# Two raw weight buffers freed in a transformer block: the second pair of each down product loads into four tiles of another pool

## The chip, the cores and the metric

The kernel runs on one core of one Trainium2 chip. The metric is the device time of one execution in microseconds. The kernel before took 1124.71 us, the median of three runs.

## What is computed

A model of two layers over 512 tokens of width 1024, in float32. Each layer has a mixing half (a gated spatial product in the first layer, attention with a forget gate in the second, both beside an attention over 256 memory rows) and a feed-forward half. Only the feed-forward half is touched:

```python
f = rmsnorm(h, ln_ffn_pre[layer])
f = (jax.nn.silu(f @ w_ffn_gate[layer]) * (f @ w_ffn_up[layer])) @ w_ffn_down[layer]
h = h + rmsnorm(f, ln_ffn_post[layer])
```

The hidden width is 2816, which is 22 blocks of 128.

## The kernel before, in words

**Parts.** Every float32 weight or activation that goes through TensorE is split into a high part (a cast on ScalarE, `whi`) and a low part (a subtraction on VectorE, `wlo`), both at line 239, and each product is three matmuls (lines 191 to 193): high by high, high by low, low by high.

**Gate and up blocks.** The first two hidden blocks are computed plainly. The other twenty are taken two at a time. For each two, a gate block and then an up block is computed by Strassen's scheme (class `Seven`): seven half-size products instead of eight. A block loads two raw weight tiles of 128x1024 (512 KB each, line 144), forms sums of their quarters on VectorE (lines 1041 to 1046), splits seven quarters or sums into parts, and runs the seven products into three banks of PSUM, named `a`, `e` and `x`. The first is product 1 into `a`, then come product 7 (which uses the sum `s3` of line 1041) into `e` and product 2 into `x`, and then the others.

**Down blocks.** Hidden blocks are grouped by four: blocks 2 to 5, 6 to 9, 10 to 13, 14 to 17. After each of these four groups a down block (`down_sevens`) multiplies the four hidden blocks, as two pairs, by the down weights, again by Strassen's scheme, once for the first pair (`a`) and once for the second (`b`). With two layers that makes eight down blocks. The last group, 18 to 21, is multiplied by other code. Each pair loads two raw tiles of 512 KB (line 1189), in which 1 KB runs of the weights lie; VectorE forms sums in place (lines 1196 to 1201), and seven products follow. Results are added to eight accumulator tiles `ys` of 128x512 in three ways: chained in PSUM, added by VectorE from PSUM (`final`, line 1226), or copied to SBUF by ScalarE (line 1221) and added by an accumulating DMA that GpSimd issues (`put`, line 1223, tile names `y<-yo`, 256 KB each, ten in a down block). The last two additions of `final`, for `shared`, go to accumulator tiles that `put` has added to before, so they must wait for those DMAs (the third and the fifth of the ten) to land.

**Buffers.** All raw weights go through one tag of four buffers:

```python
raw = wp.tile([P, 1024], F32, tag="raw", name=name("raw"), bufs=4)
```

A gate block holds two, an up block two, the pairs of a down block two each. A buffer is free again when the last part has been split from it. Separately, the pool `plain` has twelve tiles of 128x512 float32 (one tag, `y`); during the feed-forward half `ys` holds eight of them. In the first layer the four others hold the memory rows of the second layer (`mem`, four loads of 256 KB, line 345) from the beginning of the groups on.

**Order.** A scheduler fixes the order of the instructions on each engine and on SyncE's queue when the program is built. Loads of weights are all issued by SyncE, in one queue and in that order; a load that waits for its buffer holds up those behind it. Engines take their instructions strictly in order too.

I call the place where TensorE goes over from a down block to the gate block behind it a seam, and number the eight seams in order of time: one to four in the first layer (near 260, 325, 393 and 455 us), five to eight in the second (near 857, 920, 984 and 1047 us).

Of the kernel before, what the change touches and what calls it, by code (L numbers as in the profile page):

```python
# [7 lines left out]
F32 = mybir.dt.float32  # L8
# [7 lines left out]
P = 128  # L16
# [24 lines left out]
def hybrid(ctx: ExitStack, tc: tile.TileContext, i: dict, out: bass.AP):  # L41
    nc = tc.nc
# [4 lines left out]
    wp = ctx.enter_context(tc.tile_pool(name="weights", bufs=4))  # L47
# [5 lines left out]
    last_load, last_exp, last_parts = [None], [None], [None, None]  # L53

    def name(s):
        n_of[s] = n_of.get(s, 0) + 1
        return f"{s}_{n_of[s]}"
# [4 lines left out]
    def plain(s, shape=(P, T), dt=F32):  # L62
        return yp.tile(list(shape), dt, tag="y", name=name(s))

    def prob(s, shape=(P, T)):
        return tp.tile(list(shape), F32, tag="p", name=name(s), bufs=6)

    def temp(s, shape=(P, T), tag="t", bufs=4, dt=F32):
        return tp.tile(list(shape), dt, tag=tag, name=name(s), bufs=bufs)
# [4 lines left out]
    def ps(tag, shape=(P, T), s="ps"):  # L74
        return pp.tile(list(shape), F32, tag=tag, name=name(s), bufs=2 if tag == "tr" else 3)
# [1037 lines left out]
    def feed_forward(layer, phase, xp, meanwhile=None):  # L1113
# [41 lines left out]
        class Inner:  # L1155

            def __init__(self, k, aside):
                self.k, self.aside, self.u = k, aside, {}
# [22 lines left out]

        class DownSeven:

            def __init__(self, pair):
                self.x = pair.x
                raws = []
                for dh in range(2):
                    raw = wp.tile([P, 1024], F32, tag="raw", name=name("raw"), bufs=4)
                    last_load[0] = nc.sync.dma_start(
                        raw.rearrange("p (m c) -> p m c", m=4),  # L1190
                        i["w_down"][layer, 4 * dh : 4 * dh + 4, :, pair.k : pair.k + 2, :].rearrange("m p k c -> p m (k c)"))
                    raws.append(raw.rearrange("p (m k c) -> p m k c", m=4, k=2))
                a11, a12, a21, a22 = (r[:, :, x, :] for r in raws for x in range(2))
                self.w = {4: a22}
                s3 = temp("s3").rearrange("p (m c) -> p m c", m=4)
                V.tensor_sub(s3, a11, a21)
                self.w[1] = self.parts(a11)
                V.tensor_add(a21, a21, a22)
                self.w[2] = self.parts(a12)
                V.tensor_sub(a11, a11, a21)  # L1200
                V.tensor_add(a12, a11, a12)
                self.w.update({3: a12, 5: a21, 6: a11, 7: s3})
# [14 lines left out]
        def down_sevens(pairs):  # L1217

            def put(x, *where):
                some = prob("yo")  # L1220
                A.copy(some, x)  # L1221
                for tb, dh in where:
                    G.dma_start(ys[tb][dh], some, accum_op=ALU.add)  # L1223

            def final(x, tb, dh):
                V.tensor_add(ys[tb][dh], x, ys[tb][dh])  # L1226

            a, b = DownSeven(pairs[0]), None
            chain = [ps("tr", s="yc") for _ in range(2)]
            a.product(chain, 1, True, False)  # L1230
            lows = [ps("mm", s="yl") for _ in range(2)]
            a.product(lows, 2, True, False)
            shared = [ps(t, s="ys") for t in ("mm", "lg")]
            a.product(shared, 7, True, False)
            ups = [ps(t, s="yu") for t in ("lg", "lg")]
            a.product(ups, 3, True, False)
            b = DownSeven(pairs[1])
            b.product(chain, 1, False, True)
            for x in range(2):
                put(chain[x], (x, 0))  # L1240
            b.product(shared, 7, False, True)
            for x in range(2):
                put(shared[x], (x, 1), (x + 2, 1))
            for u in (a, b):
                u.product(chain, 6, False, u is b)
            for x in range(2):
                A.copy(shared[x], chain[x])
            b.product(ups, 3, False, True)
            for x in range(2):
                final(ups[x], x + 2, 0)  # L1250
            a.product(chain, 5, False, False)
            a.product(shared, 4, False, False)
            b.product(lows, 2, False, True)
            for x in range(2):
                final(lows[x], x, 0)
            b.product(chain, 5, False, True)
            for x in range(2):
                put(chain[x], (x + 2, 0), (x + 2, 1))
            b.product(shared, 4, False, True)
            for x in range(2):  # L1260
                final(shared[x], x, 1)
# [11 lines left out]
        a, close = boundary(phase, G_MIX_POST + layer, G_FFN_PRE + layer, nnorm, rb, first, evac_first, scaled)  # L1273
# [12 lines left out]
        for gi, (k0, k1) in enumerate(groups):  # L1286
            fs, pairs = [], []
            for m in range(k0, k1, 2):
                if meanwhile and m == k1 - 2 and gi == len(groups) - 1:
                    next(meanwhile)  # L1290
                if gi < len(groups) - 1:
                    pairs.append(Inner(m, m < k1 - 2))
                else:
                    fs += [(act("fhi"), act("flo")) for _ in range(2)]
                sevens((lambda: Seven(xs, lambda n: i["w_gate"][layer, m + n], "mm", gate_rows),
                        lambda: Seven(xs, lambda n: i["w_up"][layer, m + n], "lg",
                                      lambda row, t: up_rows(row, t, fs, pairs and pairs[-1]))), m == 2, m == k0)
            nk = k1 - k0
            if gi == len(groups) - 1:
                if layer:  # L1300
                    with behind([gates[2]]):
                        A.preload_act_table_set("natural_log_exp_and_others")
                if meanwhile:
                    next(meanwhile)

                eps = small("eps")
                V.tensor_mul(eps, nnorm.r4, nnorm.r4)
                V.reciprocal(eps, eps)
                V.tensor_scalar_mul(eps, eps, RMS_EPS)
                return tail_of(fs, lambda kp, dh, aside, k0=k0: down_weights(layer, k0 + 2 * kp, dh, aside), ys, eps,  # L1310
                               layer == 1)
            down_sevens(pairs)
# [300 lines left out]
```

## Time and profile before

| what | value |
|---|---|
| three runs | 1121.97, 1124.71, 1125.1 us |
| profiled execution, own time | 1122.91 us |
| its span, first to last instruction | 1121.2 us |
| mean granted TensorE clock | 0.991 |
| busy: TensorE, VectorE, ScalarE, GpSimd | 97%, 87%, 67%, 10% |
| moved by DMA | 143.84 MB, 128 GB/s on average |

A profile names instructions by engine (PE is TensorE, PEld its weight loads, DVE VectorE, ACT ScalarE, POOL GpSimd, SP SyncE), by line of the kernel and by the program's tile names. A busy TensorE is not the same as a TensorE at full pace, since matmuls overlap. The waits view adds up the idle time of an engine by what ended it: total, times, longest. The chain of waits follows the work that ended last back from the last instruction, at each step to what released it.

### The profile page before, as it was taken

What the parts mean: (1) busy time and instruction counts of PE and PEld (TensorE: products, weight loads), DVE (VectorE), ACT (ScalarE), POOL (GpSimd) and SP (SyncE); (2) the same over time, 40 slices, a digit from 0 to 9 for tenths busy, and PEclk for the clock granted to TensorE, in tenths of its full rate; (3) what the DMA queues carried; (4) which work ended last, traced back from release to release, by engine and by line L of the source; (5) the groups of instructions that cost most, each with busy time, mean ns of one, the idle gap of its engine ahead of it and who ended that gap; (6) DMA issues with size and microseconds to landing.
All of it is one profiled execution on the core that took longest, in us unless ns stands there. A gap on an engine that the chain in (4) does not pass through costs nothing.

```text
span 1121.2 us, 19822 instructions
## 1 busy us (share of the span) xinstructions
PE 1089.7 (97%) x7267; PEld 988.8 (88%) x7267; DVE 973.3 (87%) x1942; ACT 753.6 (67%) x1588; POOL 107.4 (10%) x136
## 2 busy tenths in 40 slices
PE   9999999998989999999999999999998999999998
PEld 8998889988979898898988998889997979898896
DVE  7879769998989999897968889869998989999886
ACT  7776668665656567577746788878666656666554
POOL 0000000012030112101000000000003030111200
PEclk9999999999989999999999999999999999999999
DMA  7422331338484564746222654431238464573732
GB/s 271 154 76 75 103 106 53 116 82 205 130 180 121 136 184 95 202 136 191 62 90 60 156 132 121 139 113 39 76 95 206 132 157 132 121 194 93 195 127 76
DMA packets 77849, 143.84 MB, mean 128 GB/s; under 512 B 6772, under 2 KB 41608, under 8 KB 77752
## 3 DMA queue, kind: packets, MB, share of 16 engines
q1 hardware_dynamic: 63032, 116.57, 33.3%
q0 software_dynamic: 14016, 25.70, 13.0%
q8 instruction: 57, 0.93, 0.4%
q10 hardware_dynamic: 704, 0.32, 0.1%
q14 instruction: 40, 0.33, 0.1%
HBM read 105.23 MB, written 2.10 MB: 96 GB/s over the span
## 4 chain that ended last, share of the span: by engine, by line
PE 68%; DVE 14%; DMA 11%; ACT 4%; issue 2%; POOL 1%; SPq 0%; DVEq 0%; ACTq 0%
DMA y<-yo 6%; DVE wlo L239 5%; PE y L191 4%; PE y L192 4%; PE y L193 4%; PE ps L191 4%; PE ps L193 4%; PE ps L192 4%; PE a L191 3%; PE a L192 3%; PE a L193 3%; PE e L193 3%; PE e L192 3%; PE e L191 3%; DMA raw<-in_w_down 3%; PE x L192 2%
## 5 line engine op out<-in xcount | busy, mean ns | idle before, releaser
L239 ACT CAST whi<-raw 128x512 fp32r<-128x512 f32 x492 | 287.0, 620 | 130.1 <-DVE raw L1045 46.7
L239 DVE TENSOR_TENSOR wlo<-raw,whi 128x512 fp32r<-128x512 f32 x492 | 321.0, 683 | 21.5 <-ACT whi L239 20.8
L191 PE MATMUL x<-xshi,whi 128*128 128x256 f32 x320 | 91.7, 287 | 2.0 <-DVE y L1226 1.4
L193 PE MATMUL a<-xshi,wlo 128*128 128x256 f32 x320 | 90.4, 283 | 2.0 <-DVE wlo L239 1.9
L192 PE MATMUL x<-xslo,whi 128*128 128x256 f32 x320 | 90.8, 284 | 0.0
L193 PE MATMUL x<-xshi,wlo 128*128 128x256 f32 x320 | 90.5, 283 | 0.0
L191 PE MATMUL a<-xshi,whi 128*128 128x256 f32 x320 | 89.9, 281 | 0.0
L192 PE MATMUL a<-xslo,whi 128*128 128x256 f32 x320 | 89.8, 281 | 0.0
L1223 POOL DMA_DIRECT2D y<-yo x80 | 69.4, 1149 | 211.4 <-ACT yo L1221 189.4
L191 PE MATMUL ps<-xshi,whi 128*128 128x256 f32 (+1 forms) x224 | 68.4, 305 | 0.0
L192 PE MATMUL ps<-xslo,whi 128*128 128x256 f32 (+1 forms) x224 | 66.7, 298 | 0.0
L193 PE MATMUL ps<-xshi,wlo 128*128 128x256 f32 (+1 forms) x224 | 66.3, 298 | 0.0
L191 PEld LDWEIGHTS x<-xshi,whi 128*128 128x128 f32 x320 | 61.3, 192 | 3.6 <-DVE y L1226 3.6
L193 PE MATMUL e<-t3hi,wlo 128*128 128x256 f32 x160 | 47.9, 299 | 16.7 <-DVE wlo L239 16.7
L193 PEld LDWEIGHTS a<-xshi,wlo 128*128 128x128 f32 x320 | 60.3, 188 | 3.2 <-DVE wlo L239 3.0
L193 PEld LDWEIGHTS x<-xshi,wlo 128*128 128x128 f32 x320 | 61.4, 192 | 0.0
L192 PEld LDWEIGHTS x<-xslo,whi 128*128 128x128 f32 x320 | 61.3, 192 | 0.0
L192 PEld LDWEIGHTS a<-xslo,whi 128*128 128x128 f32 x320 | 60.2, 188 | 0.4
L191 PEld LDWEIGHTS a<-xshi,whi 128*128 128x128 f32 x320 | 60.2, 188 | 0.4
L239 ACT CAST whi<-s 128x512 fp32r<-128x512 f32 x56 | 34.8, 621 | 37.0 <-DVE s L1041 30.1
L191 PE MATMUL y<-whi,mixedhi 128*128 128x512 f32 x128 | 51.3, 401 | 0.0
L192 PE MATMUL y<-wlo,mixedhi 128*128 128x512 f32 x128 | 50.6, 395 | 0.0
(352 smaller groups left out, 3584.7 us busy)
## 6 DMA issues: line engine op xcount, KB each, us to landing
raw<-in_w_gate SPq DMA_DIRECT2D x44, 512.0 KB, 3.9
raw<-in_w_up SPq DMA_DIRECT2D x44, 512.0 KB, 4.8
raw<-in_w_down SPq DMA_DIRECT2D x44, 512.0 KB, 4.6
y<-yo POOLq DMA_DIRECT2D x80, 256.0 KB, 6.7
raw<-in_w_out SPq DMA_DIRECT2D x16, 512.0 KB, 3.7
flo<-s POOLq DMA_DIRECT2D x16, 256.0 KB, 3.3
raw<-in_w_b_q SPq DMA_DIRECT2D x8, 512.0 KB, 4.3
raw<-in_w_a_v SPq DMA_DIRECT2D x6, 512.0 KB, 8.2
```

The costliest lines, as they stand in the source:

```text
L191: PE.matmul(o, w[0], x[0], start=start, stop=False, skip_group_check=more)
L192: PE.matmul(o, w[0], x[1], start=False, stop=False, skip_group_check=more)
L193: return PE.matmul(o, w[1], x[0], start=False, stop=stop, skip_group_check=more)
L239: last_parts[:] = A.copy(hi, src), (eng or V).tensor_sub(lo, src, hi)
L1223: G.dma_start(ys[tb][dh], some, accum_op=ALU.add)
```

## The change

The second pair of each down block no longer takes two raw buffers of 128x1024. It takes four tiles of 128x512 from the pool `plain`, one for each quarter of the weights, and loads them by four DMAs of 256 KB instead of two of 512 KB. In the DRAM tensor the two hidden blocks of a pair lie side by side, so a load of both reads runs of 1 KB and a load of one reads runs of 512 B. The arithmetic is the same.

```diff
-            def __init__(self, pair):
+            def __init__(self, pair, spare):
                 self.x = pair.x
-                raws = []
-                for dh in range(2):
...
-                a11, a12, a21, a22 = (r[:, :, x, :] for r in raws for x in range(2))
+                if spare:
+                    a11, a12, a21, a22 = (plain("wd").rearrange("p (m c) -> p m c", m=4) for _ in range(4))
+                    for n, a in enumerate((a11, a12, a21, a22)):
+                        last_load[0] = nc.sync.dma_start(
+                            a, i["w_down"][layer, 4 * (n // 2) : 4 * (n // 2) + 4, :, pair.k + n % 2, :].rearrange("m p c -> p m c"))
+                else:
+                    raws = []
...
-            a, b = DownSeven(pairs[0]), None
+            a, b = DownSeven(pairs[0], False), None
...
-            b = DownSeven(pairs[1])
+            b = DownSeven(pairs[1], True)
```

The lines omitted under `else` are the old ones, indented. From here on in the file, line numbers grow by six (the first pair's load is line 1195, the sum `s3` of a pair line 1202, `put` line 1229, `final` line 1232).

SyncE's queue around the second down block, before: the first pair's two loads (3907, 3909), the second pair's (3964, 3966), then the next gate block's and up block's two each.

```order
L1189 DMA raw_3907<-in_w_down 128x4x256
L1189 DMA raw_3909<-in_w_down 128x4x256
L1189 DMA raw_3964<-in_w_down 128x4x256
L1189 DMA raw_3966<-in_w_down 128x4x256
L144 DMA raw_4103<-in_w_gate 128x1024
L144 DMA raw_4105<-in_w_gate 128x1024
L144 DMA raw_4240<-in_w_up 128x1024
L144 DMA raw_4242<-in_w_up 128x1024
```

The same place now. The four loads named `wd` are the third down block's second pair; the second down block's own stand one group earlier, at the same place behind the first down block.

```order
L1195 DMA raw_3911<-in_w_down 128x4x256
L1195 DMA raw_3913<-in_w_down 128x4x256
L144 DMA raw_4111<-in_w_gate 128x1024
L144 DMA raw_4113<-in_w_gate 128x1024
L144 DMA raw_4248<-in_w_up 128x1024
L1189 DMA wd_4752<-in_w_down 128x4x128
L1189 DMA wd_4753<-in_w_down 128x4x128
L144 DMA raw_4250<-in_w_up 128x1024
L1189 DMA wd_4754<-in_w_down 128x4x128
L1189 DMA wd_4755<-in_w_down 128x4x128
```

The gate loads have moved up to the buffers of the up block before the down block, the up loads to those of the first pair, and the second pair's loads to a whole group earlier, behind the first and the second up load. In the fourth down block of the first layer, where no down block of this kind follows, the four `mem` loads stand in the place of the four `wd` loads; in the last down block of the second layer nothing does.

VectorE's order at the second seam, before: the gate block's sum `s3` (line 1041), then parts and sums, with the two additions of `shared` (line 1226) in the middle.

```order
L1041 TENSOR_TENSOR s_13_4112<-raw_4103,raw_4105 128x512
L239 TENSOR_TENSOR wlo_4115<-raw_4103,whi_4114 128x512
L1043 TENSOR_TENSOR raw_4105<-raw_4105 128x512
L239 TENSOR_TENSOR wlo_4120<-raw_4103,whi_4119 128x512
L1226 TENSOR_TENSOR y_2472<-ys_3940,y_2472 128x512
L1226 TENSOR_TENSOR y_2474<-ys_3941,y_2474 128x512
L1045 TENSOR_TENSOR raw_4103<-raw_4105,raw_4103 128x512
L239 TENSOR_TENSOR wlo_4139<-s_13_4112,whi_4138 128x512
```

And now:

```order
L1041 TENSOR_TENSOR s_13_4120<-raw_4111,raw_4113 128x512
L239 TENSOR_TENSOR wlo_4123<-raw_4111,whi_4122 128x512
L1043 TENSOR_TENSOR raw_4113<-raw_4113 128x512
L239 TENSOR_TENSOR wlo_4128<-raw_4111,whi_4127 128x512
L1232 TENSOR_TENSOR y_2472<-ys_3944,y_2472 128x512
L1232 TENSOR_TENSOR y_2474<-ys_3945,y_2474 128x512
L1045 TENSOR_TENSOR raw_4111<-raw_4113,raw_4111 128x512
L239 TENSOR_TENSOR wlo_4147<-s_13_4120,whi_4146 128x512
```

Nothing has moved there: the two additions still stand ahead of the low part of `s3`, which the product into `e` needs.

More of the change, by code (lines that the diff above doesn't have):

```diff
@@ L1182, in feed_forward @@
         class DownSeven:
-            def __init__(self, pair):
+            def __init__(self, pair, spare):
                 self.x = pair.x
-                raws = []
-                for dh in range(2):
[L1188 to L1192, printed above, removed]
-                a11, a12, a21, a22 = (r[:, :, x, :] for r in raws for x in range(2))
+                if spare:
[5 more added lines that the diff above has]
+                    raws = []
+                    for dh in range(2):
+                        raw = wp.tile([P, 1024], F32, tag="raw", name=name("raw"), bufs=4)
+                        last_load[0] = nc.sync.dma_start(
+                            raw.rearrange("p (m c) -> p m c", m=4),
+                            i["w_down"][layer, 4 * dh : 4 * dh + 4, :, pair.k : pair.k + 2, :].rearrange("m p k c -> p m (k c)"))
+                        raws.append(raw.rearrange("p (m k c) -> p m k c", m=4, k=2))
+                    a11, a12, a21, a22 = (r[:, :, x, :] for r in raws for x in range(2))
                 self.w = {4: a22}
```

## Prediction

> **What bounds the kernel now.** I read the page first, then the waits, then the chain of waits, and then the timeline at one seam.
>
> ```profile
> PE 1089.7 (97%) x7267; PEld 988.8 (88%) x7267; DVE 973.3 (87%) x1942; ACT 753.6 (67%) x1588; POOL 107.4 (10%) x136
> ```
>
> TensorE is the bound, so only what makes it wait can be won. Its weight loads (PEld) show those waits best: total, times, longest.
>
> ```profile
> PEld e L193 <- DVE wlo L239: 18.5, 9, 3.3
> ...
> PEld x L191 <- DVE y L1226: 3.6, 8, 0.9
> ...
> PEld a L193 <- DVE wlo L239: 3.0, 5, 0.9
> ```
>
> And VectorE's, for which TensorE waits there:
>
> ```profile
> DVE s L1041 <- DMA raw<-in_w_gate: 21.6, 10, 3.3
> ...
> DVE y L1226 <- DMA y<-yo: 7.3, 6, 2.2
> ...
> DVE s L1196 <- DMA raw<-in_w_down: 2.6, 7, 0.7
> ```
>
> `e`, `x` and `a` are the three banks of a gate block, and the longest wait, for the low part of `s3` into `e`, comes once at each seam:
>
> ```profile
> 267.43 0.39 PE L193 MATMUL e<-t3hi,wlo 128*128 128x256 f32 x1 [1.61 <-DVE wlo L239]
> 331.65 0.58 PE L193 MATMUL e<-t3hi,wlo 128*128 128x256 f32 x1 [3.10 <-DVE wlo L239]
> 396.19 0.39 PE L193 MATMUL e<-t3hi,wlo 128*128 128x256 f32 x1 [1.16 <-DVE wlo L239]
> 459.75 0.51 PE L193 MATMUL e<-t3hi,wlo 128*128 128x256 f32 x1 [1.91 <-DVE wlo L239]
> 860.45 0.38 PE L193 MATMUL e<-t3hi,wlo 128*128 128x256 f32 x1 [1.83 <-DVE wlo L239]
> 923.64 0.39 PE L193 MATMUL e<-t3hi,wlo 128*128 128x256 f32 x1 [2.04 <-DVE wlo L239]
> 987.40 0.39 PE L193 MATMUL e<-t3hi,wlo 128*128 128x256 f32 x1 [1.05 <-DVE wlo L239]
> 1050.46 0.58 PE L193 MATMUL e<-t3hi,wlo 128*128 128x256 f32 x1 [2.67 <-DVE wlo L239]
> ```
>
> The eight add up to 15.4 us; with 3.6 (`x`) and 3.0 (`a`), 0.8 a seam, the seams cost TensorE 22.0 us of waiting. The change removes the gate load from this. But the chain of waits, from which I take each seam's DMA link (start, length) and one link of the second pair's load, says that the gate load is last at only two seams:
>
> ```profile
> 253.89 11.51 DMA y<-yo
> ...
> 299.99 4.69 DMA raw<-in_w_down
> ...
> 317.74 11.88 DMA y<-yo
> ...
> 384.27 6.78 DMA raw<-in_w_gate
> ...
> 446.53 11.18 DMA y<-yo
> ...
> 847.30 11.12 DMA y<-yo
> ...
> 910.68 10.91 DMA y<-yo
> ...
> 975.63 6.72 DMA raw<-in_w_gate
> ...
> 1037.68 10.74 DMA y<-yo
> ```
>
> At the other six it is the fifth accumulating DMA of the down block. VectorE's timeline at the second seam shows how:
>
> ```profile
> 324.41 0.69 DVE L1041 TENSOR_TENSOR s<-raw,raw 128x512 f32<-128x512 f32 x1 [2.49 <-DMA raw<-in_w_gate]
> ...
> 329.71 0.69 DVE L1226 TENSOR_TENSOR y<-ys,y 128x512 f32<-128x512 f32 x1 [2.20 <-DMA y<-yo]
> ```
>
> VectorE waits for the gate load, then works, then stands 2.20 us in line 1226 because the DMA has landed only then; `s3`'s low part is two operations behind, and TensorE starts at 331.65. Without the first wait VectorE reaches line 1226 2.49 us sooner and stands there 2.49 us longer. So the question is when the accumulating DMAs land.
>
> **The loads that go beside them.** SyncE's queue at this seam:
>
> ```profile
> 315.98 1.51 SPq L144 DMA_DIRECT2D raw<-in_w_gate  x2
> 318.35 3.92 SPq L144 DMA_DIRECT2D raw<-in_w_up  x2
> 334.04 1.00 SPq L144 DMA_DIRECT2D raw<-in_w_gate  x2
> ```
>
> The first four are 2 MB in 6 us (the last two are for the second gate block), beside the third to sixth accumulating DMA. Afterwards the gate's 1 MB goes out a down block earlier, into the up block's buffers, and the same place holds the up's 1 MB (pieces of 4 KB) and the next second pair's 1 MB (pieces of 512 B): the same bytes at about the same times. What the pieces' size does is seen in three stretches: 236 to 238 us (loads of 1 KB pieces), 322 to 328 (4 KB pieces) and 330 to 333 (no loads). Columns: pieces, MB, share of the 16 DMA engines; q0 is the accumulating queue, q1 SyncE's.
>
> ```profile
> q0 software_dynamic: 133, 0.25, 67.4%
> q1 hardware_dynamic: 243, 0.25, 40.7%
> ```
>
> ```profile
> q0 software_dynamic: 355, 0.65, 59.0%
> q1 hardware_dynamic: 294, 1.09, 48.4%
> ```
>
> ```profile
> q0 software_dynamic: 332, 0.60, 111.1%
> ```
>
> The accumulating queue moves 0.20 MB/us alone, 0.125 beside 1 KB pieces and 0.108 beside 4 KB pieces. The third to fifth DMA are 0.786 MB: 7.3, 6.3 and 3.9 us.
>
> **The sum, part by part.**
>
> *Second pair's load.* It is now in its tiles a group earlier; the seven waits of line 1196 (2.6 us) go. They lie on the chain (the link at 299.99 is one of them), ahead of the accumulating DMAs' issue, and VectorE has no other wait there: -2.6, bounds 0 and -2.6. The operations on the new tiles are the same 128x512; I cost them at nothing.
>
> *Gate load.* Its wait (21.6 us) goes, but pays only where it is last or where the next link moves too.
>
> *Seams one, two, five, six.* Worth what the fifth DMA lands earlier. Beside the up's 4 KB pieces nothing changes. Beside 512 B pieces I have no row: if as many pieces pass per accumulating piece as at 1 KB (1.8), the loads take half as much from the queue, 0.16 MB/us is left and 4.9 us needed, 2.5 less; if as many bytes pass, 6.3 us, 1.0 less. Half of the loads are such pieces, so 1.2 or 0.5; the row nearest is the one of 1 KB pieces, read by pieces: 1.2 each, -4.8. Bounds: 0, and 3.4 (as if alone).
>
> *Seams three and seven.* Line 1226 has six waits for DMA, so here none, and the gate load is last. The e-wait goes until the accumulating DMA takes its place; with 1.2 earlier nearly all of 1.16 + 0.8 and 1.05 + 0.8: I take 1.35 each, -2.7. Bounds: 0.5 and 1.9.
>
> *Seam four.* The `mem` loads (2 KB pieces) take the place of the `wd` loads: half of 1.2, -0.6.
>
> *Seam eight.* No `wd` loads follow, so half of the loads beside the accumulating DMAs are gone: half-way between 7.3 and 3.9 us, 1.7; with the loads over before the fifth DMA begins, a little more: -2.0.
>
> *Clock.* Some of the waits cost twice. These stretches hold four of the seams; columns are TensorE's busy time, granted clock, DMA share, GB/s.
>
> ```profile
> 325.00:337.00 12.00, 8.48 (x46) 0.72 1.06 243
> 455.00:464.00 9.00, 6.91 (x41) 0.81 1.07 221
> 918.00:928.00 10.00, 7.60 (x46) 0.83 1.07 222
> 1047.00:1054.00 7.00, 4.33 (x23) 0.76 1.14 226
> ```
>
> With a clock of one half for part of each, that is 6.7, 3.4, 3.4 and 3.4 us at half clock; TensorE works through some 15 of them and loses 7.5. It happened behind e-waits of 1.91, 2.04, 2.67 and 3.10 us, not behind 1.61 and 1.83. Now the waits for `a` and `x` (0.8) merge into the e-wait: single waits of 1.6 + 0.8 - 1.2 = 1.2, 2.7, 2.1, 1.4 and 1.6 us remain at seams one, two, four, five, six, and 1.5 at eight. Two stay above 1.9, at 1.7 each: 3.4 of 7.5 lost, and for the phase of the window I keep one more: -2.4. The Trainium skill (TensorE: Matmul & The Clock Gate, "Part 1: The HAM clock gate") has the clock fall after an idle window of about 3.4 us that runs free; here 1.91 us was enough once. By the page no remaining wait would halve it and the sum would be 5.1 lower.
>
> Together 2.6 + 4.8 + 2.7 + 0.6 + 2.0 + 2.4 = 15.1 us. From the profiled execution's own 1122.9 that gives 1107.8; the median of the runs lies 1.8 above the profiled one, so 1109.6, say **1109 us**.
>
> **Cover.** The `wd` loads stand in SyncE's one queue between the two up loads and ahead of the second gate block's. Their own waits (tiles split late in the down block) hold those up. The up's second load now needs a buffer of the first pair, free earlier than the second pair's that it waited for, and its block comes only behind the gate block; the second gate block's loads went out at 334.04, 12 us behind the seam's last. Both covers are longer than the 3.5 us that the 128 small pieces of one engine take at 27 ns (worked out below). If the cover failed, the wait of line 1041 would be in the up block instead.
>
> **The rivals.**
>
> *All of it goes.* Many small pieces pass while the accumulating queue is still empty, and the rest cost it next to nothing: the fifth DMA lands 3.4 us earlier, no wait is left, no half clock. 2.6 + 22.0 + 7.5 = 32: 1092.6. For it: the row of 1 KB pieces already shows the queue gaining. Against: the up's 4 KB pieces stay. Chance 0.12.
>
> *Nothing lands earlier.* The same 2 MB go beside the DMAs; the gate load was hidden anyway. Then the second pair's 2.6, seam eight's 2.0 and its half clock 1.7, and 0.5 each at three and seven remain, 7.3, less two new half clocks of 1.7 at seams one and five, where the merged waits are 2.4 and 2.6 us: 3.9, 1120.8. Chance 0.22.
>
> *Slower.* The small pieces go in groups: SyncE's queue keeps an engine for many pieces before the accumulating queue has its turn. A 1 KB piece took 40.7% of 32 us over 243, 54 ns, a 4 KB piece 158 ns; a 512 B piece is then some 27 ns, and beyond six in a group a turn is dearer than beside 4 KB. With thirteen in a group (0.35 us) the 128 `wd` pieces of an engine are ten turns, each 0.2 us longer; what is left then goes alone, and the fifth DMA lands 1.5 us later at six seams: 9 us, and half clock at all of these, 7 more, less 2.6 and seam eight's 3.7: 1134. Against: beside 1 KB pieces only 1.8 passed per turn. Chance 0.11. The Trainium skill (DMA: Bandwidth & Descriptors, "Queues, rings and completion order") says so: an engine drains a packet of typically 9 to 17 descriptors from one queue before it switches; by the row above the trace does not agree for 1 KB pieces, and no row has 512 B ones.
>
> That the tiles are not free and the change does nothing is excluded: the loads stand a group ahead.
>
> **How the numbers follow.** The forecast has 0.55. Its own range is 1097 (the fifth DMA 2.5 us earlier: 10.0 + 3.8 + 1.2 + 2.5 + 2.6 + 7.5 = 27.6) to 1115 (0.5 earlier: 2.0 + 1.6 + 0.3 + 2.0 + 2.6 + 1.0 = 9.5). The range of 8 in 10 takes in nothing landing earlier and half of the way to all going: 1094 to 1123. A measurement of this kernel tells about 0.3% from no change, 3.4 us, so faster begins below 1121.3. The case at 1120.8 lies on that edge; a third of it counts as faster, the rest as the same. Faster 0.55 + 0.12 + 0.08 = 0.75, same 0.14, slower 0.11.
>
> **What would show it.** Right: line 1041 no longer waits at a seam and line 1196 not at all; line 1226 waits at five or six seams, 2 to 4 us each, and the chain has `y<-yo` links there that are about 1 us shorter; beside `wd` pieces the accumulating queue moves over 0.108 MB/us; one to three stretches of half clock. Wrong: the links are as long as now or longer, line 1226 has taken over the whole of the 21.6 us, and the half clock has come to more seams; or the line 1041 waits have moved to the up blocks.

## The result and the profile after

| kernel | median us | runs | ratio to the kernel before | 95% interval |
|---|---|---|---|---|
| before | 1124.9 | 1121.97 to 1126.37 | | |
| changed | 1107.84 | 1105.52 to 1110.95 | 0.9853 | 0.982 to 0.9886 |
| changed, once more (e5), beside other experiments | 1104.83 | 1103.97 to 1110.45 | 0.9814 | 0.978 to 0.9848 |

Each ratio is to the kernel before as it was measured beside the same group of runs (its median was 1128.61 us beside e1 to e4, 1125.51 beside e5 to e8 and 1127.02 beside e9 to e11), so ratios compare better than medians. For e5 a ratio of 0.982 to 0.989 was expected; it came out just below.

The forecast was 1109 us, with a range of 1094 to 1123. The profiled execution of the changed kernel has an own time of 1105.52 us, a span of 1103.8 (17.4 less than before) and a granted clock of 0.995.

The page's first row, TensorE's waits and VectorE's waits, of the changed kernel:

```profile
PE 1082.3 (98%) x7266; PEld 986.1 (89%) x7267; DVE 972.7 (88%) x1942; ACT 752.5 (68%) x1588; POOL 107.5 (10%) x136
```

```profile
PEld e L193 <- DVE wlo L239: 14.0, 7, 3.2
```

```profile
DVE y L1232 <- DMA y<-yo: 13.1, 7, 3.4
...
DVE s L1041 <- DMA raw<-in_w_gate: 1.8, 2, 0.9
```

TensorE's busy time fell from 1089.7 to 1082.3 with the same matmuls. Some 2.4 us of that is the clock (worked out below), since a matmul at half clock is busy for longer; the rest must be waits too short for the page to count as idle, for by the start times of the matmuls (also below) the two kernels differ only at the seams and in the down blocks. The rows for `x` (3.6) and `a` (3.0) are gone, `e` went from 18.5 to 14.0. On VectorE the 21.6 us for the gate load became 1.8, the 2.6 of the second pair's load have no row any more, and the wait for the accumulating DMAs rose from 7.3 to 13.1: part of the old wait was only moved.

The e-waits, seam by seam, from TensorE's timeline (seams seven and eight have none now):

```profile
265.06 0.39 PE L193 MATMUL e<-t3hi,wlo 128*128 128x256 f32 x1 [0.57 <-DVE wlo L239]
327.62 0.58 PE L193 MATMUL e<-t3hi,wlo 128*128 128x256 f32 x1 [2.74 <-DVE wlo L239]
390.08 0.39 PE L193 MATMUL e<-t3hi,wlo 128*128 128x256 f32 x1 [0.89 <-DVE wlo L239]
452.90 0.39 PE L193 MATMUL e<-t3hi,wlo 128*128 128x256 f32 x1 [2.96 <-DVE wlo L239]
850.96 0.39 PE L193 MATMUL e<-t3hi,wlo 128*128 128x256 f32 x1 [1.57 <-DVE wlo L239]
913.32 0.39 PE L193 MATMUL e<-t3hi,wlo 128*128 128x256 f32 x1 [2.50 <-DVE wlo L239]
```

They add up to 11.2 us, against 15.4 + 6.6 before. (The row of 14.0 us is that of the weight loads; its seventh wait lies inside the last group of the first layer, at 487 us.) Two of them are longer than before (seams four and six, 1.91 and 2.04 there), which fits if the small waits for `x` and `a` in front of them are counted too: these merged into the one wait that is left.

At the seams the chain of waits has these DMA links now (start, length):

```profile
254.38 8.63 DMA y<-yo
315.02 10.56 DMA y<-yo
378.62 9.43 DMA y<-yo
440.05 10.81 DMA y<-yo
839.33 9.59 DMA y<-yo
900.91 10.37 DMA y<-yo
```

All are the fifth accumulating DMA. At five of the six seams where it was on the chain before, the links are 0.4 to 2.9 us shorter; at seam three it has taken the gate load's place; at seven and eight there is no such link. VectorE at the second seam:

```profile
319.12 0.69 DVE L1041 TENSOR_TENSOR s<-raw,raw 128x512 f32<-128x512 f32 x1
...
321.86 0.69 DVE L1232 TENSOR_TENSOR y<-ys,y 128x512 f32<-128x512 f32 x1 [0.24 <-PE ys L193]
325.68 0.69 DVE L1232 TENSOR_TENSOR y<-ys,y 128x512 f32<-128x512 f32 x1 [3.12 <-DMA y<-yo]
```

Line 1041 waits for nothing, and line 1232 stands for 3.12 us where it stood for 2.20: of the 2.49 us that VectorE no longer waits for the gate load, 0.92 come back here.

### The profile page after: what moved, and what is told of

It is laid out like the page before. It is cut to its first block, busy times and chain, and to the rows that moved or that the text cites. A ratio compares the mean times of both kernels' runs of the same rounds, so it can differ in the third digit from the quotient of the medians.

```text
span 1103.8 us, 19831 instructions
## 1 busy us (share of the span) xinstructions
PE 1082.3 (98%) x7266; PEld 986.1 (89%) x7267; DVE 972.7 (88%) x1942; ACT 752.5 (68%) x1588; POOL 107.5 (10%) x136
## 3 DMA queue, kind: packets, MB, share of 16 engines
q0 software_dynamic: 14016, 25.70, 13.1%
## 4 chain that ended last, share of the span: by engine, by line
PE 77%; DVE 10%; DMA 6%; ACT 3%; issue 2%; POOL 1%; SPq 0%; DVEq 0%; ACTq 0%
DMA y<-yo 5%; PE y L191 5%; PE y L192 5%; PE y L193 4%; PE a L191 4%; PE a L192 4%; PE a L193 4%; PE ps L191 4%; PE ps L193 4%; PE ps L192 4%; PE e L193 3%; DVE wlo L239 3%; PE e L192 3%; PE e L191 3%; PE x L192 3%; PE x L193 3%
## 5 line engine op out<-in xcount | busy, mean ns | idle before, releaser
L239 ACT CAST whi<-raw 128x512 fp32r<-128x512 f32 x444 | 260.4, 619 | 116.1 <-DVE raw L1045 46.2
L239 DVE TENSOR_TENSOR wlo<-raw,whi 128x512 fp32r<-128x512 f32 x444 | 291.9, 687 | 20.4 <-ACT whi L239 19.8
L239 ACT CAST whi<-s 128x512 fp32r<-128x512 f32 x56 | 34.8, 622 | 24.6 <-DVE s L1041 15.4
## 6 DMA issues: line engine op xcount, KB each, us to landing
wd<-in_w_down SPq DMA_DIRECT2D x32, 256.0 KB, 10.5
```

Source lines behind the costliest of these rows:

```text
L239: last_parts[:] = A.copy(hi, src), (eng or V).tensor_sub(lo, src, hi)
```

## The experiments

**Theory.** A seam ends when the fifth accumulating DMA lands, and the loads that share the 16 DMA engines with it set when. The change gained by freeing the gate load, by what the loads now leave to that DMA, and by fewer stretches of half clock. **Rivals.** Only the freed buffers matter; or the queue of small pieces is harmful; or the DMA's issue, not its neighbours, sets the landing.

| run | edit to the changed kernel | median us | ratio | 95% interval |
|---|---|---|---|---|
| e1 | `wd` loads later | 1098.74 | 0.9727 | 0.9693 to 0.976 |
| e2 | up loads held | 1134.3 | 1.0057 | 1.0033 to 1.008 |
| e3 | order of the accumulating DMAs | 1092.55 | 0.9674 | 0.9649 to 0.97 |
| e4 | up loads in 512 B pieces | 1099.54 | 0.9733 | 0.9706 to 0.976 |
| e6 | kernel *before* with the order of e3 | 1111.17 | 0.9857 | 0.9825 to 0.9888 |
| e7 | second pair late again | 1125.61 | 1.0 | 0.9979 to 1.002 |
| e8 | TensorE kept busy in three waits | 1109.47 | 0.9846 | 0.9821 to 0.987 |
| e9 | the same, products in the old order | 1109.01 | 0.9849 | 0.9808 to 0.989 |
| e10 | e1 and e3 together | 1090.0 | 0.9671 | 0.965 to 0.9692 |
| e11 | e10 and `mem` loads later | 1089.11 | 0.9664 | 0.9639 to 0.9689 |

e1 to e4 ran beside one another, then e6 to e8 beside the changed kernel's second measurement (0.9814), then e9 to e11. One thousandth is 1.1 us.

### e1: the wd loads out of the way

```diff
-                        last_load[0] = nc.sync.dma_start(
-                            a, i["w_down"][...])
+                        with behind([loads[-3]]):
+                            last_load[0] = nc.sync.dma_start(
+                                a, i["w_down"][...])
```

`loads` lists the loads of gate and up blocks; the third from the end is the second gate block's last.

> The changed kernel with the four wd loads issued behind the second gate block's loads, so that no 512 B piece goes beside the accumulating DMAs at seams one to three and five to seven; the mem loads at seam four stay. Theory (a seam ends when the fifth accumulating DMA lands, and the loads that share the 16 DMA engines with it set when): the e-waits of 0.73, 2.90, 1.05, 1.73 and 2.66 us at seams one, two, three, five and six become nearly nothing, as at seam eight where no wd load stands now, and two of the three stretches of half clock (1.7 us each) go: 9.1 + 3.4 = 12.5 us less than the changed kernel, about 1095; seam four keeps its 3.1. Rival (the up block's 4 KB pieces hold the DMA, not the wd loads, or its issue by GpSimd does): nothing moves, 1106 to 1110.

Measured: 1098.74 us. TensorE's and VectorE's waits:

```profile
PEld e L196 <- DVE wlo L242: 10.1, 8, 3.6
```

```profile
DVE y L1236 <- DMA y<-yo: 9.5, 8, 3.4
```

The e-wait at seam two fell from 2.7 to under 0.9 us and at seam six from 2.5 to 0.4; at seam four, where the `mem` loads stayed, it is the 3.6. One stretch of half clock is left, at seam four, and the median time from issue to landing of the `y<-yo` DMAs fell from 7.4 to 5.6 us. The link of the second seam, which began at 315.02 us and was 10.56 long, is now this:

```profile
314.71 8.58 DMA y<-yo
```

It begins 0.3 us earlier and ends 2.3 earlier: the neighbours of the DMA set its landing, and the rival that its issue does is excluded. The time fell by less than expected (about 1095). VectorE still waits 0.8 to 1.2 us for the DMA at seams two, three, five and six, and at seam three the e-wait did not fall at all (0.89 to 1.10); that the 4 KB pieces are the cause of what stays is argued, not shown.

### e2: the up loads held

```diff
+        if y is not None:
+            G.tensor_copy(raw[:, :1], y[:, :1])
```

`y` is the tile of the last addition of line 1232 (`ys[1][1]`).

> The changed kernel with the first up block's loads of a group held until the last addition of line 1232 before it has been made (a one-column copy by GpSimd into the raw tile, which is then overwritten, reads that accumulator tile and the load waits for the copy). The wd loads then stand ahead of the up loads in SyncE's queue, beside the accumulating DMAs as now. Theory: only 512 B pieces are left beside the third to fifth accumulating DMA, at 0.164 MB/us for 0.786 MB, 4.8 us, against some 5.8 now (half beside 4 KB pieces at 0.108, half at 0.164): 1.0 less at five or six seams, 0.7 at the first, and one or two stretches of half clock, 1.7 each: 1099 to 1102. Rival (the wd loads alone hold the DMA): 1106 to 1110.

Measured: 1134.3, a miss of over 30 us. The wait for `y<-yo` has gone from VectorE's list, as the theory has it, but ScalarE and TensorE show what came instead:

```profile
ACT whi L241 <- DMA raw<-in_w_up: 44.6, 9, 6.3
```

```profile
PEld a L193 <- ACT s L1073: 17.3, 8, 3.4
...
PEld a L195 <- DVE wlo L241: 11.3, 11, 1.7
```

At the second seam the held loads were issued at 331.60 us, and ScalarE stood up to 6.3 us for them. The parts of the up block are made well ahead of its products; a load that is in time for TensorE is late for the engines that work ahead. This is a cover that my prediction had counted as long ("its block comes only behind the gate block"): from TensorE's side it is, from ScalarE's it isn't. About the pieces this run tells nothing.

### e3: the two awaited DMAs first

```diff
             for x in range(2):
-                put(shared[x], (x, 1), (x + 2, 1))
+                put(shared[x], (x, 1))
+            for x in range(2):
+                G.dma_start(ys[x + 2][1], yo[x], accum_op=ALU.add)
```

> The changed kernel with the four accumulating DMAs of shared issued in the order of use: both that line 1232 waits for as the third and the fourth, the two others as the fifth and the sixth. Theory: the queue moves one DMA after the other, so the one that is waited for lands one DMA of 262 KB earlier, 1.6 us at 0.164 MB/us to 2.4 us at 0.108; the e-waits of 0.73, 2.90, 1.05, 3.12, 1.73 and 2.66 us lose 0.73, 1.8, 1.05, 1.8, 1.7 and 1.8, 8.9 together, and the three stretches of half clock 3 to 5: 12 to 14 us less, about 1095. Rival (the DMAs in the queue share the engines and land close together): under 0.3 us a seam, 1106 to 1108.

Measured: 1092.55, 0.9674. The waits and the second seam:

```profile
PEld e L193 <- DVE wlo L239: 5.1, 4, 1.6
```

```profile
324.89 0.69 DVE L1235 TENSOR_TENSOR y<-ys,y 128x512 f32<-128x512 f32 x1 [1.53 <-DMA y<-yo]
```

The wait of 3.12 became 1.53, one 262 KB DMA earlier as expected, and at seams one, three, five the e-wait is gone. No half clock is left at any seam. The DMAs of this queue land one after the other, and the fifth was what a seam waited for.

### e4: the up loads in small pieces

```diff
+            for x in range(2):
+                last_load[0] = nc.sync.dma_start(
+                    raw.rearrange("p (j x c) -> p x j c", x=2, c=P)[:, x], src.rearrange("p (j x c) -> p x j c", x=2, c=P)[:, x])
```

> The changed kernel with the first up block's two loads of a group as four, each of alternate runs of 512 B, so that the pieces beside the accumulating DMAs are all of 512 B and none of 4 KB; the same bytes at the same places in SyncE's queue. Theory (about one load piece passes per accumulating piece, so small pieces take less): the accumulating queue moves 0.164 MB/us throughout where it moved 0.108 for about half the time, the fifth DMA lands some 1.0 us earlier at six seams (0.7 at the first), and one or two stretches of half clock go: 1099 to 1103. Rival one (an engine takes 9 to 17 descriptors of one queue before it turns to the other): 128 more small pieces for each engine make ten turns 0.2 us longer each, 1.5 us later at six seams, half clock at more of them: about 1119. Rival two (bytes count, not pieces): 1106 to 1110.

Measured: 1099.54. In a stretch at seam two (319 to 324 us; pieces, MB, share of the engines):

```profile
q0 software_dynamic: 412, 0.75, 83.7%
q1 hardware_dynamic: 654, 0.33, 27.7%
```

The accumulating queue moved 0.150 MB/us beside 512 B pieces (0.108 beside 4 KB), and 1.6 load pieces passed for each of its own, small ones of 34 ns (27.7% of 80 us over 654). The times of both rivals, 1119 with 9 to 17 descriptors in a turn and 1106 to 1110 if bytes count, are out. A price came too: the up loads take longer, and one block at 850 us waited 2.86 us for its parts behind a load.

### e6: the order alone, on the kernel before

The edit of e3 on the kernel before.

> The kernel before with the other order of the accumulating DMAs alone (both that line 1226 waits for issued third and fourth). Theory (two things end a seam there, the gate load and the fifth accumulating DMA, and either alone hides part of the other's gain): the waits of line 1226, 7.3 us at six seams, go, and with them two to four stretches of half clock, 1.7 us each; the waits for the gate load, 21.6 us in line 1041, stay, and are last everywhere: 10 to 14 us less than before, a ratio of 0.988 to 0.991, and 18 to 20 us behind the changed kernel with that order. Rival (only the accumulating DMAs matter, and the gate load was hidden anyway): the ratio is that of the changed kernel with that order, 0.967 to 0.972.

Measured: 1111.17, 0.9857, a little more than was expected (0.988 to 0.991). Two of the stretches of half clock are left, at 267 and 854 us. VectorE's waits for DMAs are these, and none for `y<-yo`:

```profile
DVE s L1041 <- DMA raw<-in_w_gate: 23.5, 10, 3.3
...
DVE s L1196 <- DMA raw<-in_w_down: 3.2, 7, 0.6
```

The chain has no `y<-yo` link. Every down block but the first has a link for its second pair's load, and every seam but the first one for its gate load; the first two:

```profile
300.69 4.89 DMA raw<-in_w_down
318.05 7.33 DMA raw<-in_w_gate
```

So before the change two things ended a seam, and where the DMA came last it cost 2.2 us more at most (the longest wait of line 1226). The order alone is worth 14 thousandths, the buffers alone 15 to 19, both together 33. The rival, by which the order would have brought all of it, is out. Whether each hides a part of the other's gain stays open: with 15 the sum falls short by 4, with 19 by nothing.

### e7: the second pair late again

```diff
+                G.tensor_copy(mark, w[1][:, :1])
...
+                        G.tensor_copy(a[:, 0, :1], mark)
+                        with behind(after):
```

> The changed kernel with the second pair's loads put back to where they were before, behind the first pair's of the same down block and not sooner than the last split of the up block ahead of it (a one-column copy by GpSimd that reads that split, then one into each wd tile, which the load overwrites). The buffers stay as changed, so the gate loads still come early, and no wd load is left beside the accumulating DMAs; it is to be held against the kernel with late wd loads (ratio 0.9727), which has the seams the same and the second pair early. Theory: the seven waits of line 1202 come back, 2.6 us together, as the loads land at the last moment: a ratio higher by 0.0023 than 0.9727, about 0.975. Rival (the second pair's wait was hidden or was given back at once): no difference, 0.972 to 0.973.

Measured: 1125.61, 1.0. The hold was far too strong:

```profile
DVE s L1209 <- DMA wd<-in_w_down: 24.6, 8, 4.0
```

That is 3.1 us at each of eight down blocks, where the kernel before had 0.4. Against e1 that cost 26.9 us by the medians and 31 by the ratios, of which four stretches of half clock more (five against one) are some 6. So a microsecond of this wait costs about 0.85 to 1 us, and 1.1 to 1.25 with the clock; the expected 2.6 us can't be read from this run, but that such a wait lies on the path can.

### e8 and e9: keeping TensorE busy

```diff
+                for _ in range(self.fill):
+                    PE.matmul(self.q, self.w2[0][:, :P], self.xs[2][0][0], start=True, stop=True)
```

> The changed kernel with fourteen matmuls more (128x128 by 128x256, on operands at hand, into bank e, which product 7 then overwrites) between product 2 and product 7 of the gate block at seams two, four and six, where the three stretches of half clock are; at 118 ns each they fill 1.65 of the 2.7 to 3.1 us that TensorE waits there. Theory (the half clock follows TensorE's own idleness and costs 1.7 us a stretch): no stretch is left, the waits end when they did, and the two high-part matmuls of product 7 that stood ahead of the wait cost 0.2 us each time behind it: 4.4 us less than the changed kernel, a ratio lower by 0.004. Rival (the stretches cost nothing, since the matmuls behind a seam have slack, or they come from the wait's end and not from TensorE's idleness): no gain, 0 to 1 us more.

> The fourteen extra matmuls of the run before, at the same three seams, but with the order of the products kept: behind the first half of product 2 and ahead of product 7, whose copy then has the second half of product 2 and product 6 to hide behind, as in the changed kernel. Theory (the half clock follows TensorE's idleness, 1.7 us a stretch): the waits for the copy of bank e go, no stretch of half clock is left at seams two, four and six, and the time is 4 to 6 us below the changed kernel's, a ratio 0.004 to 0.005 lower than the one beside the run before (0.9814): 0.976 to 0.978. Rival (the stretches cost nothing): 0.981 to 0.983.

Measured: 1109.47 and 1109.01, 0.9846 and 0.9849 beside 0.9814: no gain in either. In e8 product 7 stands behind product 2, and product 4, the next into bank `e`, waits until ScalarE has copied product 7 out of it; two stretches of half clock remain, at 334 and 853 us:

```profile
PEld e L191 <- ACT s L1078: 6.5, 5, 2.0
```

In e9 no stretch is left. Granted clock (0.50 or 1.00, the seventh column behind the stretch) of the changed kernel and of e9 behind the waits of seams two, four and six:

```profile
327.61:331.02 3.41, 3.40 (x16) 3.40 (x17) 3.41 (x6) 2.52 (x7) 0.67 (x1) 0.50 1.14 235
453.91:457.32 3.41, 3.41 (x18) 3.41 (x17) 3.41 (x7) 2.13 (x5) 0.23 (x1) 0.50 1.13 211
914.71:918.12 3.41, 3.41 (x18) 3.41 (x17) 3.41 (x7) 1.64 (x4) 0.00 (x0) 0.50 1.12 219
390.10:393.50 3.40, 3.40 (x29) 3.40 (x29) 3.40 (x6) 3.18 (x8) 0.86 (x1) 1.00 1.15 238
```

```profile
328.30:331.70 3.40, 3.35 (x28) 3.36 (x29) 3.40 (x6) 3.01 (x7) 0.71 (x1) 1.00 1.13 230
453.10:456.50 3.40, 3.35 (x28) 3.36 (x28) 3.40 (x6) 1.90 (x5) 0.87 (x1) 1.00 1.12 203
911.80:915.20 3.40, 3.31 (x28) 3.32 (x29) 3.40 (x7) 3.06 (x7) 0.86 (x1) 1.00 1.14 221
```

In 3.4 us TensorE has 28 or 29 matmuls at full clock (the fourth row of the changed kernel is seam three, undisturbed) and 16 to 18 at half: some 12 matmuls of 0.118 us, 1.4 to 1.5 us a stretch. So the stretches come from TensorE's idleness and have a price. Yet the kernel did not get faster, and e9's waits show one reason:

```profile
PEld e L191 <- ACT s L1082: 2.9, 5, 0.7
PEld yu L191 <- ACT whi L239: 2.5, 2, 1.3
...
PEld yc L191 <- ACT yo L1235: 2.4, 6, 0.8
```

The first two have no such row in the changed kernel and the third is 1.1 there: that is 6.7 us, more than the three stretches cost together. Where the time went can be seen when the profiled executions of the changed kernel and of e9 are laid side by side, matmul by matmul: the three filled seams are 4.7 us shorter (1.4 to 1.7 each, near the price above), and the rest of the kernel is 5.9 us longer (2.2 at the other seams, 1.1 in the down blocks, 2.7 elsewhere). That the new order on ScalarE and VectorE, to which the extra matmuls led the scheduler, is the cause of the 5.9 is argued, not shown.

### e10 and e11: together

e10 has the edits of e1 and e3. In e11 the loads of line 345 are issued `with behind(loads[-1:])`, and the memory rows' work begins behind the next gate block.

> The changed kernel with both edits that paid: wd loads behind the second gate block's loads, and the two accumulating DMAs that are waited for issued third and fourth. Theory (the same wait is shortened twice, so what is left after the other order is all that the late loads can win): the e-waits left with the other order at seams two and six, 1.30 and 0.61 us, go; seam four (1.46, mem loads) stays: 1.9 us less than the 1092.55 of the other order alone, a ratio of 0.9655 against 0.9674. Rival (the gains add up, 12.6 and 18 thousandths): a ratio of about 0.955, 1075.

> The kernel with late wd loads and the other order, and besides the four mem loads at seam four put behind the next gate block's loads too (the work on the memory rows then begins one block later). Theory: the e-wait of 1.46 us at seam four goes as well: 1.5 us less than the run without, a ratio lower by 0.0013, about 0.964, and no wait for an accumulating DMA left over 0.5 us at any seam. Rival (the first up block's loads, 4 KB pieces that stay, hold the DMA at this seam): the e-wait at seam four stays over 1.2 us.

Measured: 1090.0 and 1089.11, 0.9671 and 0.9664. The two edits do not add up (0.955 would be the sum): they shorten the same wait, as the theory says; over e3 the time is 2.5 us lower, but the ratios can't be told apart. In e10 the e-wait at seam four is 1.5 us on TensorE's timeline, in e11 it has gone; its one row is a wait inside the last group, at 475 us:

```profile
PEld e L196 <- DVE wlo L242: 1.2, 1, 1.2
```

VectorE's wait for the DMA at that seam, in e10 and in e11:

```profile
443.37 0.69 DVE L1239 TENSOR_TENSOR y<-ys,y 128x512 f32<-128x512 f32 x1 [1.88 <-DMA y<-yo]
```

```profile
441.33 0.69 DVE L1240 TENSOR_TENSOR y<-ys,y 128x512 f32<-128x512 f32 x1 [0.21 <-DMA y<-yo]
```

e11 has the lowest median here, though its ratio can't be told from those of e10 and e3. Against the changed kernel nearly all of the gain is the order of e3; against the kernel before, about half is the freed buffers.

## Why the prediction was right

The likeliest case came true, and its terms sum to nearly the right size (1107.84 us against 1109):

| term | forecast | measured | from |
|---|---|---|---|
| second pair's load | -2.6 | -2.9 | rows below |
| seams one, two, five, six | -4.8 | -4.4 | e-waits, with 0.8 a seam for `a` and `x` before |
| seams three, seven | -2.7 | -2.9 | the same |
| seam four | -0.6 | +0.2 | 1.91 + 0.8 to 2.96 |
| seam eight | -2.0 | -3.5 | 2.67 + 0.8 to 0 |
| clock | -2.4 | -2.4 | 17.1 us at half clock (72 matmuls) to 10.2 (48), 0.1 us each |
| sum | -15.1 | -15.9 | span: -17.4 |

The table counts waits, and mixes those of the weight loads (`a`, `x`) with those of the matmuls (`e`), as the forecast did. A second count needs neither: the order of the matmuls is all but the same in both kernels, so their start times can be laid side by side. The changed kernel gains 3.0 us in the eight down blocks and, from the last matmul of a down block to 18 us behind it, 2.9, 2.2, 0.9, 0.3, 1.7, 0.4, 1.7 and 4.5 us at the eight seams, the clock in it: 14.5 where the forecast had 12.5. Elsewhere the two differ by 0.1 us in sum. So the 1.5 us that the table lacks lie at the seams.

Part of the agreement is an average. I gave 1.2 us to each of seams one, two, five and six; by the e-waits they gained 1.8, 1.2, 1.1 and 0.3. And the noise is of the size of the small terms: the same kernel profiled a second time had a span 4.9 us longer, with 16.7 us of e-waits where the first has 14.0.

*Second pair.* TensorE's waits inside the down blocks, before and after the change:

```profile
PEld ys L191 <- ACT fhi L239: 4.5, 6, 1.3
...
PEld yc L192 <- DVE wlo L239: 3.2, 4, 0.9
...
PEld ys L192 <- DVE wlo L239: 1.8, 5, 0.8
...
PEld yc L191 <- ACT yo L1221: 1.5, 8, 0.2
...
PEld yu L192 <- DVE wlo L239: 0.7, 2, 0.5
```

```profile
PEld ys L191 <- ACT fhi L239: 3.6, 6, 1.2
PEld yc L192 <- DVE wlo L239: 2.7, 4, 1.0
...
PEld ys L192 <- DVE wlo L239: 1.4, 6, 0.3
...
PEld yc L191 <- ACT yo L1227: 1.1, 6, 0.2
```

11.7 became 8.8, near the 2.6 that VectorE had waited and the 3.0 of the start times, and the `raw<-in_w_down` links of the chain are gone.

*Seams.* The step on which most hung was that loads of 512 B pieces leave the accumulating queue 0.16 MB/us. Between 259 and 263 us, `wd` loads beside it:

```profile
q0 software_dynamic: 374, 0.67, 91.4%
q1 hardware_dynamic: 344, 0.18, 21.3%
```

0.168 MB/us: right, though by two errors that partly cancel. I had 1.8 load pieces of 27 ns pass per accumulating piece; here it is 0.9, and each took 40 ns (21.3% of 64 us over 344). At seam two, where both kinds of pieces stand beside it, the queue moved 0.79 MB from 321 to 327 us, 0.13 MB/us, between the 0.108 and the 0.164 of the forecast. Line 1232 waits at six seams as foreseen, but 0.7 to 3.4 us each and not 2 to 4. The rule that the Trainium skill gives (DMA: Bandwidth & Descriptors, "Queues, rings and completion order"), 9 to 17 descriptors from one queue in a turn, made the rival of 1134; neither that time came, nor the 1119 of e4. The length of a turn itself is not shown: I took the row of 1 KB pieces as evidence against the rule, but turns of many pieces on both sides would give the same counts.

*Seam four* failed: "half of 1.2" for the 2 KB `mem` pieces was too much, there is next to no gain (0.3 us by the start times). e11 shows that these loads held the DMA there, since without them the wait is gone. *Seam eight* was mis-sized: without `wd` loads it reached the bound that I had put for a DMA alone, 3.4.

*Clock.* The stretch at seam eight vanished and the long one at seam two became a short one. Behind 1.57 us nothing happened, behind 2.50 and more each time. The idle window of about 3.4 us that the Trainium skill gives (TensorE: Matmul & The Clock Gate, "Part 1: The HAM clock gate") would have left no stretch; the trace has three, behind waits of 2.50 to 2.96 us. The number of stretches came out as forecast, but the third was not one that the waits gave: I had added it for the phase of the window, and it came at seam six, where 2.50 us of wait stayed and not 1.6.

*Rivals.* "All of it goes" needed the 4 KB pieces away as well; e3 and e11 reach that place (1092.6 was its time) by another way. "Nothing lands earlier" is refuted by the shorter links. *Cover:* no engine waited for a `wd` load, and line 1041 does not wait in the up blocks.

## What to carry to other kernels

When a wait is removed, look for what lands next, and ask what shares its way: here the second wait was a DMA slowed by the very loads that had been moved. The cheapest gain was neither a buffer nor a load but the order of issue in that queue: what is waited for first goes first. And a load is due when the first engine that prepares it needs it, not when the bound engine does.

## What the runs showed of the hardware

- The accumulating DMAs issued by GpSimd land one after the other: issuing the awaited one a place earlier ended its wait 1.6 us sooner (3.12 to 1.53).
- Small pieces beside such a queue hurt it less than large ones: 0.168 MB/us beside mostly 512 B `wd` pieces, 0.150 where all were 512 B, 0.108 beside 4 KB, 0.20 alone. But loads in 512 B pieces (34 to 40 ns each) are slow themselves: the `wd` DMAs took 10.5 us from issue to landing (median) for 256 KB, and 7.2 out of the seams (e1), where the raw loads of 512 KB before took 3.9 to 4.8.
- TensorE's clock fell to one half for 3.41 us, or twice that. In the changed kernel's trace this came with each wait of 2.50 us and more, but the length of a single wait does not decide it: the clock did not fall behind one of 2.88 us (e2, at 871 us) or of 2.59 (e7, at 467), and it fell behind two of 0.72 and 1.06 us close together (e6, at 267).
- The stretches of one trace begin whole multiples of 3.413 us apart, as on a fixed grid: in the kernel before at 330.16, 459.86, 924.08 and 1050.37 us (38, 136 and 37 times), in the changed one at 327.61, 453.91 and 914.71 (37 and 135 times). What counts is how long TensorE ran no matmul within one window of this grid, in one piece or several. Of the windows at full clock in the thirteen traces (without their first and last 15 us), all 17 that held 2.0 us or more without a matmul were followed by half clock, none of those with less than 1.66, and 6 of the 12 between. An edge of the grid cut the 2.88 us of e2 in two, with 1.91 in one window; the two short waits of e6 fell into one, with 1.76 together.
